# Hybrid attention block on one core: the order of four engines written out for the start of the kernel, extra matmuls while data arrive, mask building moved behind the last weight split

## The chip, the cores and the metric

The kernel runs on one core of one Trainium2 chip. The metric is the device time of one execution, in microseconds. The kernel before takes 1032.24 us (median of 3 runs, 1032.16 to 1032.51).

## The reference

One decoder block on 512 tokens of width 1024, all in float32:

```
h    = RMSNorm(x)                      # over 1024, gain norm1_g
proj = h @ W_in                        # 1024 x 9744
A    = dilated attention, 3 groups of 8 heads of 64; q and k are RMS-normed per head
B    = gated linear attention, 4 heads, output norm, swish gate
mix  = sigmoid(gA) * (A @ W_A) + sigmoid(gB) * (B @ W_B)
x    = x + mix @ W_out
x    = x + relu(RMSNorm(x) @ W_up)^2 @ W_down
```

Only the very beginning matters here: `RMSNorm(x)`, and the first 512 columns of `W_in`, which are the queries of attention group 0, followed by their normalisation per head (`q = q * rsqrt(mean(q^2) + eps)`), while the keys of group 0, the next 512 columns at `kind * 1536`, are multiplied.

## The kernel before

**Precision.** Each float32 factor is split into a high part (`hi`, a copy rounded to fp32r by ScalarE, line 110) and a low part (`lo = raw - hi`, line 111). A product is three matmuls: hi*hi, hi*lo, lo*hi (lines 155 to 157 with a whole projection's loop around them). So each weight piece of 128 x 1024 needs one ScalarE copy `whi` and one subtraction `wlo`. For the first four pieces `wlo` is made by GpSimd, for all later ones by VectorE. `whi` and `wlo` have four buffers each, the raw weights `wraw` two.

**Tiles.** The 512 tokens are four tiles of 128 (`i` = 0..3). A projection by `mm_tok` has four PSUM banks of the tag `mm`, one per token tile, and goes over 8 blocks of 128 rows of the weight: 8 x 4 x 3 = 96 matmuls of 512 columns. The tag `mm` has five banks in all, the tag `aux` three.

**The beginning, per token tile `i`.** `square_in`: ScalarE squares x and sums. `rsqrt`: a chain of small steps, VectorE (`rv`), ScalarE (`ry`, logarithm and exponential), VectorE (`r`). `scale_in`: VectorE multiplies x by `r` and the gain, in two halves. The gain row is spread over the partitions by two TensorE matmuls (`g1b`). `turn_in`: TensorE transposes h, 8 times 128 x 128. `parts_in`: ScalarE copies the high part `hTh` from PSUM, VectorE subtracts for the low part `hTl`. Beside it `split_in` makes `whi` and `wlo` of the first projection's four weight pieces. In this stretch the order on ScalarE and VectorE is as the program writes it (`manual_schedule`); TensorE and GpSimd are ordered by the scheduler's own estimate.

**Constants.** The block behind `issue_after(last.ins)` loads small columns by GpSimd DMAs and builds the attention masks and the masks of the gated attention on GpSimd. It may be issued only once `last`, the last low part of h, has been scheduled; on GpSimd the scheduler then laid it between the `wlo` of the first projection.

**After the first projection** (`qkv`, kind 0, that is q): per token tile ScalarE copies the bank to `rw` (which frees the bank), GpSimd squares it (`s2`, line 346), VectorE sums per head (`ss`), then the `rsqrt` chain, VectorE scales (`s2` again), and four transposes (`turn`, line 357) go into TensorE's order while the next projection (k) is under way, the first of them after 48 of its 96 matmuls.

**What sets the order.** Each engine takes its instructions in one fixed order and waits on semaphores. The build fixes that order; from the first projection's end on it is the scheduler's.

Of the kernel before, what the change touches and what calls it, by code (L numbers as in the profile page):

```python
# [8 lines left out]
F32 = mybir.dt.float32  # L9
# [7 lines left out]
P = 128  # L17
# [24 lines left out]
def kernel(ctx: ExitStack, tc: tile.TileContext, x, norm1_g, w_in, q_g, k_g,  # L42
# [54 lines left out]
        return t  # L97


    n_split = [0]  # L100
    first = []
    later = []
    turns = []

    def split(raw_ap, shape):
        hi = ring.tile([P] + shape, F32R, name="whi", tag="whi")
        lo = ring.tile([P] + shape, F32R, name="wlo", tag="wlo")
        n_split[0] += 1
        with tc.high_priority() if n_split[0] > 4 else nullcontext():
            act(hi, raw_ap, AF.Copy)  # L110
            (nc.vector if n_split[0] > 4 else nc.gpsimd).tensor_tensor(lo, raw_ap, hi.bitcast(F32), OP.subtract)  # L111
        return hi, lo

    def raw_load(w, r0, nk, c0, n):
# [29 lines left out]
    def mm_tok(w, c0, lhs, r0=0, nk=KB):  # L144

        banks = [mm_bank() for _ in range(NT)]
        for k4 in range(0, nk, 4):
            raw = None if first else raw_load(w, r0 + k4 * P, 4, c0, 512)
            for k2 in range(0, 4, 2):
                hi, lo = first.pop(0) if raw is None else split(raw[:, k2:k2 + 2], [2, 512])  # L150
                for kk in range(2):
                    k = k4 + k2 + kk
                    for i in range(NT):
                        lh, ll = lhs(k, i)
                        nc.tensor.matmul(banks[i], lh, hi[:, kk], start=(k == 0), stop=False)  # L155
                        nc.tensor.matmul(banks[i], lh, lo[:, kk], start=False, stop=False)  # L156
                        mm = nc.tensor.matmul(banks[i], ll, hi[:, kk], start=False, stop=(k == nk - 1))  # L157
                    if later and k in (3, 4, 5, 6):
                        with tc.issue_after(mm.ins):
                            later.pop(0)()  # L160
        return banks
# [34 lines left out]
    raws = [slot(10 + j, [P, 4, 512], f"raw{j}") for j in range(2)]  # L196


    def load_x(i):
        nc.sync.dma_start(xs[i // 2][:, i % 2], x[i * P:(i + 1) * P])  # L200

    def load_in(j):
        nc.sync.dma_start(raws[j // 2][:, j % 2 * 2:j % 2 * 2 + 2],
                          w_in[2 * j * P:2 * (j + 1) * P, 0:512].rearrange("(k p) n -> p k n", p=P))

    g1r = slot(8, [P, D], "g1r")[0:1]
    nc.scalar.dma_start(g1r, norm1_g)
    for i in range(NT):
        load_x(i)
        load_in(i)  # L210

    one_r = small.tile([1, P], F32, name="one_r", tag="one_r", bufs=1)
    nc.vector.memset(one_r, 1.0)
    g1b = [mm_bank(), aux()]
    for j in range(2):
        nc.tensor.matmul(g1b[j], one_r, g1r[:, j * 512:(j + 1) * 512], start=True, stop=True)

    ss4 = consts.tile([P, 4], F32, name="ss4")
    r4 = consts.tile([P, 4], F32, name="r4")

    def square_in(i):
        act(hs[i // 2][:, i % 2], xs[i // 2][:, i % 2], AF.Square, accum_out=ss4[:, i:i + 1])

    def scale_in(i):
        for j in range(2):
# [1 line left out]
            nc.vector.scalar_tensor_tensor(hs[i // 2][:, i % 2, cs], xs[i // 2][:, i % 2, cs], r4[:, i:i + 1],  # L227
                                           g1b[j], op0=OP.mult, op1=OP.mult)

    def turn_in(i):  # L230
        bs = [aux() for _ in range(2)]
        for k in range(KB):
            nc.tensor.transpose(bs[k // 4][:, k % 4 * P:(k % 4 + 1) * P], hs[i // 2][:, i % 2, k * P:(k + 1) * P],
                                ident)
        return [b.rearrange("p (k t) -> p k t", k=4) for b in bs]

    def parts_in(i, bs):
        for j in range(2):
            dh = hT.hi[j][:, :, i * P:(i + 1) * P]
            act(dh, bs[j], AF.Copy)  # L240
            last = tt(hT.lo[j][:, :, i * P:(i + 1) * P], bs[j], dh.bitcast(F32), OP.subtract)
        return last

    def split_in():
        j = len(first)
        first.append(split(raws[j // 2][:, j % 2 * 2:j % 2 * 2 + 2], [2, 512]))

    with tc.manual_schedule(engines={mybir.EngineType.Activation, mybir.EngineType.DVE}):
        square_in(0)
        rsqrt(r4[:, 0:1], ss4[:, 0:1], D, 1)  # L250
        scale_in(0)
        split_in()
        square_in(1)
        rsqrt(r4[:, 1:2], ss4[:, 1:2], D, 1)
        b0 = turn_in(0)
        scale_in(1)
        parts_in(0, b0)
        split_in()
        square_in(2)
        square_in(3)  # L260
        rsqrt(r4[:, 2:4], ss4[:, 2:4], D, 2)
        b1 = turn_in(1)
        scale_in(2)
        parts_in(1, b1)
        split_in()
        b2 = turn_in(2)
        scale_in(3)
        parts_in(2, b2)
        split_in()
        last = parts_in(3, turn_in(3))  # L270


    with tc.issue_after(last.ins):
        qk_cols = consts.tile([P, 2], F32, name="qk_cols")
        for j, g in enumerate((q_g, k_g)):
            for hf in range(2):
                nc.gpsimd.dma_start(qk_cols[hf * E:(hf + 1) * E, j:j + 1], g.rearrange("o e -> e o"))
        gqk = consts.tile([P, 1], F32, name="gqk")
        nc.vector.scalar_tensor_tensor(gqk, qk_cols[:, 0:1], float(E) ** -0.5, qk_cols[:, 1:2],
                                       op0=OP.mult, op1=OP.mult)  # L280

        gqk2 = consts.tile([P, 2], F32, name="gqk2")
        nc.vector.memset(gqk2, 0.0)
        for hf in range(2):
            nc.vector.tensor_copy(gqk2[hf * E:(hf + 1) * E, hf:hf + 1], gqk[hf * E:(hf + 1) * E])

        mask_a = consts.tile([P, 256], F32, name="mask_a")
        nc.gpsimd.memset(mask_a, 0.0)
        nc.gpsimd.affine_select(mask_a[:, :P], mask_a[:, :P], pattern=[[1, P]], compare_op=OP.is_ge,
                                fill=NEG, base=0, channel_multiplier=-1)  # L290
        nc.gpsimd.affine_select(mask_a[:, P:], mask_a[:, P:], pattern=[[-1, P]], compare_op=OP.is_ge,
                                fill=NEG, base=0, channel_multiplier=1)
        mask_b = consts.tile([P, 256], F32, name="mask_b")
        nc.gpsimd.tensor_copy(mask_b[:, :P], mask_a[:, P:])
        dist = t2k(P, "dist", I32)
        nc.gpsimd.iota(dist, pattern=[[1, P]], base=P, channel_multiplier=-1)
        nc.vector.tensor_single_scalar(dist, dist, 3, op=OP.bitwise_and)
        far = t2k(P, "far")
        nc.vector.tensor_copy(far, dist)
        nc.vector.tensor_scalar(far, far, 0.5, NEG, op0=OP.is_gt, op1=OP.mult)  # L300
        tt(mask_b[:, P:], far, mask_a[:, P:], OP.min)


        def block_mask(name, w, segs):

            g = consts.tile([P, w], U8, name=name)
            f = work_e.tile([P, w], F32, name="f", tag="s2", bufs=2)
            nc.gpsimd.memset(f, 1.0)
            for off, ng, nx, gr, r0, nr in segs:
                v = f[:, off:off + ng * nx].rearrange("p (g x) -> p g x", x=nx)  # L310
                nc.gpsimd.affine_select(v, v, pattern=[[-gr, ng], [0, nx]], compare_op=OP.is_ge, fill=0.0,
                                        base=-r0, channel_multiplier=1)
                nc.gpsimd.affine_select(v, v, pattern=[[gr, ng], [0, nx]], compare_op=OP.is_ge, fill=0.0,
                                        base=r0 + nr - 1, channel_multiplier=-1)
            nc.gpsimd.tensor_copy(g, f)
            return g

        pair_mask = {m: block_mask(f"pm{m}", 256, [(64 * i, 64 // m, m, 2 * m, 0, m) for i in range(NT)])
                     for m in (1, 32)}
        quad_mask = {}  # L320
        for m in (2, 8):
            G = 32 // m
            quad_mask[m] = block_mask(f"qm{m}", 384, [
                (192 * i + off, G, (3 - a) * m, 4 * m, a * m, m)
                for i in range(2) for a, off in enumerate((0, 96, 160))])
        gbias = col("gbias", gate_bias, GH)
        og_col = col("og_col", out_g, 2)
        bb_col = col("bb_col", branch_bias, 16)
        n2_col = col("n2_col", norm2_g, KB)
        nbb_col = consts.tile([P, 16], F32, name="nbb_col")  # L330
        nc.vector.tensor_scalar_mul(nbb_col, bb_col, -1.0)


    def qkv(g, lhs, sq, sk, sv):
# [1 line left out]

        res = []
        for kind, ss_ in ((0, sq), (1, sk)):
            banks = mm_tok(w_in, kind * 1536 + g * 512, lhs)
            dst = [slot(s, [P, 4, S], f"a{kind}{g}{n}") for n, s in enumerate(ss_)]  # L340
            for i in range(NT):
                rw = work_e.tile([P, 512], F32, name="rw", tag="rw", bufs=4)
# [584 lines left out]
```

## Time and profile before

| | |
|---|---|
| median of 3 runs | 1032.24 us |
| profiled execution: its time, its span | 1034.02 us, 1032.3 us |
| TensorE busy | 1012.2 us, 98% |
| VectorE, ScalarE, GpSimd busy | 64%, 49%, 8% |
| TensorE on the chain that ended last | 92% |

TensorE is nearly always busy, and where it is not, is almost all in the first 21 us. A time line row gives the start, the duration, the engine, the source line, the operation with its output and inputs, and in brackets the idle time of that engine just before and what ended it. A row "x3" merges three alike instructions that follow each other; its duration is that of all three. Matmuls overlap, so the pace is read from their starts, not from their durations.

### The profile page before, as it was taken

Reading aid. Unit: us, or ns where it says so; the run is one execution under the profiler, and the core shown is the slowest. Engines: PE = TensorE matmul, PEld = TensorE weight load, DVE = VectorE, ACT = ScalarE, POOL = GpSimd, SP = SyncE. Lnnn points to the kernel's source line nnn. Section 1 sums busy time; section 2 is a strip of 40 time slices with the busy share of each in tenths; the row PEclk is TensorE's granted clock in tenths of the full one; section 3 lists DMA queues with packets and bytes.
Section 4 is the critical chain, followed back from the end, with each engine's and each line's share of the span. In section 5 each row is a group of like instructions: output and inputs, shape, how many; then the busy total and the mean of one; then the engine's idle time right before and its main releaser. Section 6 shows DMA issues by size and latency. Waiting matters only on the chain.

```text
span 1032.3 us, 12479 instructions
## 1 busy us (share of the span) xinstructions
PE 1012.2 (98%) x4772; PEld 860.3 (83%) x4772; DVE 665.7 (64%) x1109; ACT 507.3 (49%) x845; POOL 81.8 (8%) x116
## 2 busy tenths in 40 slices
PE   5999999999999999999999999999999999999998
PEld 3888999999988788788888888777888888888886
DVE  5654454435444623989856657985885895796695
ACT  4345443433544423765646863365544554563552
POOL 7510001001000000010002200000000000000000
PEclk8999999999999999999999999999999999999999
DMA  6132102332201223212212334252143134225102
GB/s 244 45 109 93 42 5 78 96 109 82 82 12 34 92 69 116 82 43 80 64 60 85 120 123 163 79 207 82 42 156 114 57 98 146 83 82 163 41 1 81
DMA packets 63788, 91.84 MB, mean 89 GB/s; under 512 B 3249, under 2 KB 37041, under 8 KB 63730
## 3 DMA queue, kind: packets, MB, share of 16 engines
q1 hardware_dynamic: 61520, 87.59, 25.6%
q10 hardware_dynamic: 1794, 3.18, 0.9%
q8 instruction: 37, 0.61, 0.2%
q0 software_dynamic: 416, 0.28, 0.2%
q14 instruction: 21, 0.17, 0.1%
HBM read 88.92 MB, written 2.13 MB: 88 GB/s over the span
## 4 chain that ended last, share of the span: by engine, by line
PE 92%; DVE 4%; ACT 1%; POOL 1%; issue 1%; DMA 0%; SPq 0%; POOLq 0%; DVEq 0%
PE mm L136 11%; PE mm L137 10%; PE mm L138 10%; PE mm L155 10%; PE mm L157 9%; PE mm L156 9%; PE mm L759 4%; PE mm L758 4%; PE mm L760 4%; PE aux L400 3%; PE aux L759 2%; PE aux L760 2%; PE aux L758 2%; PE aux L423 1%; PE aux L394 1%; PE aux L409 1%
## 5 line engine op out<-in xcount | busy, mean ns | idle before, releaser
L111 DVE TENSOR_TENSOR wlo<-wraw,whi 128x1024 fp32r<-128x1024 f32 x127 | 157.5, 1240 | 145.7 <-ACT whi L78 144.0
L78 ACT ACTIVATE whi<-wraw 128x1024 fp32r<-128x1024 f32 x127 | 134.3, 1057 | 189.5 <-PE mm L157 85.5
L155 PE MATMUL mm<-whi,hTh 128*128 128x512 f32 x416 | 172.0, 414 | 1.6 <-ACT hTh L78 1.5
L156 PE MATMUL mm<-wlo,hTh 128*128 128x512 f32 x416 | 167.1, 402 | 3.8 <-POOL wlo L111 3.8
L157 PE MATMUL mm<-whi,hTl 128*128 128x512 f32 x416 | 168.1, 405 | 0.0
L156 PEld LDWEIGHTS mm<-wlo,hTh 128*128 128x128 f32 x416 | 103.0, 248 | 12.7 <-POOL wlo L111 4.2
L155 PEld LDWEIGHTS mm<-whi,hTh 128*128 128x128 f32 x416 | 102.8, 247 | 10.8 <-ACT hTh L78 2.3
L157 PEld LDWEIGHTS mm<-whi,hTl 128*128 128x128 f32 x416 | 102.6, 247 | 9.0
L136 PE MATMUL mm<-xgh,whi 128*128 128x512 f32 x240 | 93.4, 389 | 0.0
L137 PE MATMUL mm<-xgl,whi 128*128 128x512 f32 x240 | 93.4, 389 | 0.0
L138 PE MATMUL mm<-xgh,wlo 128*128 128x512 f32 x240 | 93.4, 389 | 0.0
L758 PE MATMUL mm<-whi,left 128*128 128x512 f32 x200 | 78.0, 390 | 0.7 <-ACT whi L78 0.7
L759 PE MATMUL mm<-wlo,left 128*128 128x512 f32 x200 | 77.8, 390 | 0.5 <-DVE wlo L111 0.5
L136 PE MATMUL mm<-hTh,whi 128*128 128x512 f32 x192 | 77.6, 404 | 0.0
L760 PE MATMUL mm<-whi,left 128*128 128x512 f32 x200 | 77.2, 389 | 0.0
L137 PE MATMUL mm<-hTl,whi 128*128 128x512 f32 x192 | 76.4, 398 | 0.0
L138 PE MATMUL mm<-hTh,wlo 128*128 128x512 f32 x192 | 76.3, 398 | 0.0
L78 ACT ACTIVATE whi<-traw 128x1024 fp32r<-128x1024 f32 x40 | 42.3, 1058 | 46.1 <-PE mm L760 22.3
L81 DVE TENSOR_TENSOR left<-tmp,left 128x256 fp32r<-128x256 f32 (+1 forms) x40 | 43.2, 1089 | 22.8 <-ACT left L78 22.6
L78 ACT ACTIVATE p<-p,nmx 128x256 f32<-128x256 f32 (+1 forms) x64 | 31.2, 488 | 51.3 <-DVE nmx L388 51.3
L396 DVE COPY pt<-aux 128x512 f32<-128x512 f32 (+1 forms) x32 | 21.1, 659 | 54.8 <-PE aux L394 54.6
L136 PEld LDWEIGHTS mm<-xgh,whi 128*128 128x128 f32 x240 | 45.0, 188 | 9.4
(249 smaller groups left out, 1892.8 us busy)
## 6 DMA issues: line engine op xcount, KB each, us to landing
wraw<-in_w_in_dram SPq DMA_DIRECT2D x36, 1024.0 KB, 5.0
wraw<-in_w_ff_up_dram SPq DMA_DIRECT2D x16, 1024.0 KB, 5.3
traw<-in_w_ff_down_dram SPq DMA_DIRECT2D x12, 1024.0 KB, 5.5
wraw<-in_w_gla_branch_dram SPq DMA_DIRECT2D x4, 1024.0 KB, 5.0
wraw<-in_w_ff_down_dram SPq DMA_DIRECT2D x4, 1024.0 KB, 5.0
traw<-in_w_out_dram SPq DMA_DIRECT2D x3, 1024.0 KB, 6.9
x<-in_x_dram SPq DMA_DIRECT2D x4, 512.0 KB, 7.6
raw<-in_w_in_dram SPq DMA_DIRECT2D x4, 512.0 KB, 8.0
```

Of the source, the lines that this page charges most:

```text
L78: nc.scalar.activation(o, i, f, **kw)
L81: return nc.vector.tensor_tensor(o, a, b, op)
L111: (nc.vector if n_split[0] > 4 else nc.gpsimd).tensor_tensor(lo, raw_ap, hi.bitcast(F32), OP.subtract)
L136: nc.tensor.matmul(b, hi[:, k], rh, start=(k == 0), stop=False)
L137: nc.tensor.matmul(b, hi[:, k], rl, start=False, stop=False)
L138: mm = nc.tensor.matmul(b, lo[:, k], rh, start=False, stop=(k == nk - 1))
L155: nc.tensor.matmul(banks[i], lh, hi[:, kk], start=(k == 0), stop=False)
L156: nc.tensor.matmul(banks[i], lh, lo[:, kk], start=False, stop=False)
L157: mm = nc.tensor.matmul(banks[i], ll, hi[:, kk], start=False, stop=(k == nk - 1))
L758: nc.tensor.matmul(banks[i], lh, hi[:, jk], start=f, stop=False, skip_group_check=True)
L759: nc.tensor.matmul(banks[i], lh, lo[:, jk], start=False, stop=False, skip_group_check=True)
L760: nc.tensor.matmul(banks[i], ll, hi[:, jk], start=False, stop=l, skip_group_check=True)
```

## The change

The order of all four compute engines is written out until the last `wlo` of the first projection, that projection included (`first_mm`); `mm_tok` no longer has a special case for it. The four x tiles are loaded ahead of the weights on SyncE's queue, with the first weight piece on ScalarE's queue. 25 matmuls of 256 columns whose results are not read (`keep_busy`) stand before the gain's matmuls (15) and between the first two transposed tiles (10). `g1b` takes two `mm` banks. The first `wlo` is made by VectorE, the other three by GpSimd, one after the other. The block of constants and masks waits for the last of these three (`last_g`) as well.

```diff
     def split(raw_ap, shape):
...
-        n_split[0] += 1
-        with tc.high_priority() if n_split[0] > 4 else nullcontext():
+        with tc.high_priority():
             act(hi, raw_ap, AF.Copy)
-            (nc.vector if n_split[0] > 4 else nc.gpsimd).tensor_tensor(lo, raw_ap, hi.bitcast(F32), OP.subtract)
+            tt(lo, raw_ap, hi.bitcast(F32), OP.subtract)
...
     nc.scalar.dma_start(g1r, norm1_g)
+    load_in(nc.scalar, 0)
     for i in range(NT):
-        load_x(i)
-        load_in(i)
-
+        nc.sync.dma_start(xs[i // 2][:, i % 2], x[i * P:(i + 1) * P])
+    for j in (1, 2, 3):
+        load_in(nc.sync, j)
...
+    def keep_busy(n, b):
+
+        for m in range(n):
+            nc.tensor.matmul(b[:, :256], busy[:, m % 4 * P:m % 4 * P + P], busy[:, :256], start=True, stop=True)
...
+    def split_in(j, eng):
+        raw = raws[j // 2][:, j % 2 * 2:j % 2 * 2 + 2]
...
+        act(hi, raw, AF.Copy)
+        first_w.append((hi, lo))
+        return eng.tensor_tensor(lo, raw, hi.bitcast(F32), OP.subtract)
...
+    with tc.manual_schedule(engines={ET.Activation, ET.DVE, ET.Pool, ET.PE}):
+
+        g1b = [mm_bank(), mm_bank()]
+        first_banks = [mm_bank(), mm_bank()]
+        keep_busy(15, first_banks[1])
+        for j in range(2):
+            nc.tensor.matmul(g1b[j], one_r, g1r[:, j * 512:(j + 1) * 512], start=True, stop=True)
         square_in(0)
-        rsqrt(r4[:, 0:1], ss4[:, 0:1], D, 1)
+        rsq(0, 1)
         scale_in(0)
-        split_in()
         square_in(1)
-        rsqrt(r4[:, 1:2], ss4[:, 1:2], D, 1)
-        b0 = turn_in(0)
+        b0 = turn_in(0, [aux(), aux()])
+        high_in(0, b0)
+        rsq(1, 2)
         scale_in(1)
-        parts_in(0, b0)
-        split_in()
+        keep_busy(10, first_banks[1])
+        b1 = turn_in(1, [aux(), mm_bank()])
+        low_in(0, b0)
+        split_in(0, nc.vector)
         square_in(2)
+        high_in(1, b1)
+        low_in(1, b1)
+        first_mm(0, [0])
+        first_mm(1, [0])
         square_in(3)
-        rsqrt(r4[:, 2:4], ss4[:, 2:4], D, 2)
-        b1 = turn_in(1)
+        rsq(2, 4)
+        split_in(1, nc.gpsimd)
         scale_in(2)
-        parts_in(1, b1)
-        split_in()
-        b2 = turn_in(2)
+        b2 = turn_in(2, [aux(), aux()])
+        high_in(2, b2)
         scale_in(3)
-        parts_in(2, b2)
-        split_in()
-        last = parts_in(3, turn_in(3))
-
-
-    with tc.issue_after(last.ins):
+        low_in(2, b2)
+        b3 = turn_in(3, [aux(), mm_bank()])
+        first_banks += [mm_bank(), mm_bank()]
+        first_mm(0, [1])
+        first_mm(1, [1])
+        split_in(2, nc.gpsimd)
+        high_in(3, b3)
+        last = low_in(3, b3)
+        last_g = split_in(3, nc.gpsimd)
+        first_mm(2, [0, 1])
+        first_mm(3, [0, 1])
+        for j in (2, 3):
+            for i in range(NT):
+                first_mm(i, [j])
+
+
+    with tc.issue_after(last.ins), tc.issue_after(last_g.ins):
         qk_cols = consts.tile([P, 2], F32, name="qk_cols")
...
-            banks = mm_tok(w_in, kind * 1536 + g * 512, lhs)
+            banks = first_banks if kind == g == 0 else mm_tok(w_in, kind * 1536 + g * 512, lhs)
```

The rest of the kernel stands as before. What the new code does to three places of the built order:

On GpSimd, at the start of the kernel, before (`wlo` is a low part of the first projection's weights, the rest are constants and masks):

```order
masks.py:199 AFFINE_SELECT ident<-ident 128x128
L111 TENSOR_TENSOR wlo<-raw_97,whi 128x1024
L277 DMA qk_cols<-in_attn_q_norm_g_dram 64x1
L277 DMA qk_cols<-in_attn_k_norm_g_dram 64x1 x2
L288 MEMSET mask_a 128x256
L296 IOTA dist 128x128
L289 AFFINE_SELECT mask_a<-mask_a 128x128
```

The same place now:

```order
masks.py:199 AFFINE_SELECT ident<-ident 128x128
L256 TENSOR_TENSOR wlo<-raw_97,whi 128x1024
L256 TENSOR_TENSOR wlo<-raw_98,whi 128x1024 x2
L320 DMA qk_cols<-in_attn_q_norm_g_dram 64x1 x2
L320 DMA qk_cols<-in_attn_k_norm_g_dram 64x1 x2
L331 MEMSET mask_a 128x256
L339 IOTA dist 128x128
```

The three `wlo` that GpSimd still has stand ahead of all mask work, where before there were four, spread through it.

On GpSimd, ahead of the first square of q (`s` <- `rw`), before:

```order
L96 DMA n_col<-in_norm_g_dram 128x8x1
L313 AFFINE_SELECT f<-f 128x64
L313 AFFINE_SELECT f<-f 128x32
L315 CAST qm_296<-f 128x384
L111 TENSOR_TENSOR wlo<-raw_98,whi 128x1024
L346 TENSOR_TENSOR s_427<-rw 128x512
```

The same place now:

```order
L354 AFFINE_SELECT f<-f 128x32
L96 DMA n_col<-in_norm_g_dram 128x8x1
L356 AFFINE_SELECT f<-f 128x64
L356 AFFINE_SELECT f<-f 128x32
L358 CAST qm_425<-f 128x384
L389 TENSOR_TENSOR s_456<-rw 128x512
```

What stands directly ahead of the square of q is now the last mask, and no longer the last `wlo`.

On ScalarE, where the first projection ends (`whi` <- `wraw` belongs to the k projection, `rw` <- `mm` frees a bank of q, `ry` is the chain of the normalisation of q's first token tile), before:

```order
L78 ACTIVATE whi<-wraw 128x1024 x3
L78 ACTIVATE rw<-mm 128x512 x3
L78 ACTIVATE ry<-rv 128x8
L78 ACTIVATE rw<-mm 128x512
L78 ACTIVATE whi<-wraw 128x1024
L78 ACTIVATE ry<-ry 128x8
```

The same place now:

```order
L78 ACTIVATE whi<-wraw 128x1024 x3
L78 ACTIVATE rw<-mm 128x512 x2
L78 ACTIVATE ry<-rv 128x8
L78 ACTIVATE ry<-ry 128x8
L78 ACTIVATE rw<-mm 128x512 x2
L78 ACTIVATE whi<-wraw 128x1024
```

Two copies of q's banks stand ahead of the `ry` chain now, where before there were three.

## Rows read from the trace of the kernel before

**Rows 1.** Page, parts 1 and 4: engines, and the chain that ended last.

```profile
PE 1012.2 (98%) x4772; PEld 860.3 (83%) x4772; DVE 665.7 (64%) x1109; ACT 507.3 (49%) x845; POOL 81.8 (8%) x116
PE 92%; DVE 4%; ACT 1%; POOL 1%; issue 1%; DMA 0%; SPq 0%; POOLq 0%; DVEq 0%
```

**Rows 2.** Time line of TensorE (start us, us, ... [idle before <- releaser]).

```profile
13.45 1.12 PE L233 MATMUL aux<-ident,h 128*128 128x128 f32 x4 [0.92 <-DVE hTl L81]
...
16.77 0.40 PE L155 MATMUL mm<-whi,hTh 128*128 128x512 f32 x1
20.96 0.80 PE L156 MATMUL mm<-wlo,hTh 128*128 128x512 f32 x1 [3.79 <-POOL wlo L111]
...
35.45 0.39 PE L156 MATMUL mm<-wlo,hTh 128*128 128x512 f32 x1
...
46.11 0.39 PE L155 MATMUL mm<-whi,hTh 128*128 128x512 f32 x1
...
56.99 0.60 PE L357 MATMUL aux<-ident,s 128*128 128x128 f32 x4
```

**Rows 3.** Windows of 1 us: busy per engine, granted clock, DMA share, GB/s.

```profile
20.00:21.00 1.00, 0.04 (x1) 0.04 (x1) 0.97 (x2) 0.17 (x1) 1.00 (x2) 0.50 0.01 2
...
26.00:27.00 1.00, 1.00 (x7) 0.95 (x6) 0.69 (x1) 0.32 (x2) 1.00 (x4) 0.59 0.00 0
27.00:28.00 1.00, 1.00 (x6) 0.78 (x5) 0.45 (x1) 1.00 (x2) 1.00 (x4) 1.00 0.00 0
```

**Rows 4.** Time line of GpSimd, 0 to 50 us.

```profile
1.36 0.73 POOL L277 DMA_DIRECT2D qk_cols<-in_attn_q_norm_g_dram  x1 [0.35 <-issue]
...
9.57 0.55 POOL L277 DMA_DIRECT2D qk_cols<-in_attn_q_norm_g_dram  x1
...
18.55 2.36 POOL L111 TENSOR_TENSOR wlo<-raw,whi 128x1024 fp32r<-128x1024 f32 x1
20.85 0.40 POOL L315 CAST pm<-f 128x256 uint8<-128x256 f32 x1
...
28.34 1.19 POOL L96 DMA_DIRECT2D bb_col<-in_branch_gate_bias_dram  x1
...
30.91 2.38 POOL L111 TENSOR_TENSOR wlo<-raw,whi 128x1024 fp32r<-128x1024 f32 x1
33.26 1.09 POOL L313 TENSOR_SCALAR_AFFINE_SELECT f<-f 128x96 f32<-128x96 f32 x4
...
36.67 2.39 POOL L111 TENSOR_TENSOR wlo<-raw,whi 128x1024 fp32r<-128x1024 f32 x1
44.94 2.04 POOL L346 TENSOR_TENSOR s<-rw 128x512 f32<-128x512 f32 x2 [5.88 <-ACT rw L78]
```

**Rows 5.** Time line of ScalarE, 0 to 50 us.

```profile
8.96 1.06 ACT L78 ACTIVATE h<-x 128x1024 f32<-128x1024 f32 x1 [1.77 <-DMA x<-in_x_dram]
...
10.67 1.07 ACT L78 ACTIVATE hTh<-aux 128x512 fp32r<-128x512 f32 x2
11.62 1.06 ACT L78 ACTIVATE whi<-raw 128x1024 fp32r<-128x1024 f32 x1
...
17.82 0.20 ACT L78 ACTIVATE ry<-rv 128x2 f32<-128x2 f32 x1 [2.64 <-DVE rv L184]
...
44.27 1.96 ACT L78 ACTIVATE rw<-mm 128x512 f32<-128x512 f32 x3 [2.29 <-PE mm L157]
47.04 0.21 ACT L78 ACTIVATE ry<-rv 128x8 f32<-128x8 f32 x1 [0.82 <-DVE rv L184]
47.16 0.58 ACT L78 ACTIVATE rw<-mm 128x512 f32<-128x512 f32 x1
```

**Rows 6.** Time line of VectorE, 0 to 50 us.

```profile
11.38 0.75 DVE L227 SCALAR_TENSOR_TENSOR h<-x,r,mm 128x512 f32<-128x512 f32 x1
...
12.70 1.29 DVE L81 TENSOR_TENSOR hTl<-aux,hTh 128x512 fp32r<-128x512 f32 x2
...
34.60 1.23 DVE L111 TENSOR_TENSOR wlo<-wraw,whi 128x1024 fp32r<-128x1024 f32 x1
```

More of the change, by code (lines that the diff above doesn't have):

```diff
@@ L97, in col @@
         return t
-    n_split = [0]
-    first = []
     later = []
@@ L147, in mm_tok @@
         for k4 in range(0, nk, 4):
-            raw = None if first else raw_load(w, r0 + k4 * P, 4, c0, 512)
+            raw = raw_load(w, r0 + k4 * P, 4, c0, 512)
             for k2 in range(0, 4, 2):
-                hi, lo = first.pop(0) if raw is None else split(raw[:, k2:k2 + 2], [2, 512])
+                hi, lo = split(raw[:, k2:k2 + 2], [2, 512])
                 for kk in range(2):
@@ L196, with load_in, rsq @@
     raws = [slot(10 + j, [P, 4, 512], f"raw{j}") for j in range(2)]
[L199 to L204, printed above, removed]
+    def load_in(eng, j):
+        eng.dma_start(raws[j // 2][:, j % 2 * 2:j % 2 * 2 + 2],
+                      w_in[2 * j * P:2 * (j + 1) * P, 0:512].rearrange("(k p) n -> p k n", p=P))
     g1r = slot(8, [P, D], "g1r")[0:1]
     nc.scalar.dma_start(g1r, norm1_g)
+    load_in(nc.scalar, 0)
     for i in range(NT):
-        load_x(i)
-        load_in(i)
+        nc.sync.dma_start(xs[i // 2][:, i % 2], x[i * P:(i + 1) * P])
+    for j in (1, 2, 3):
+        load_in(nc.sync, j)
     one_r = small.tile([1, P], F32, name="one_r", tag="one_r", bufs=1)
     nc.vector.memset(one_r, 1.0)
-    g1b = [mm_bank(), aux()]
-    for j in range(2):
-        nc.tensor.matmul(g1b[j], one_r, g1r[:, j * 512:(j + 1) * 512], start=True, stop=True)
+    busy0 = slot(9, [P, 512], "busy0")
+    nc.vector.memset(busy0, 1.0)
+    busy = slot(12, [P, 512], "busy", F32R)
+    nc.vector.tensor_copy(busy, busy0)
     ss4 = consts.tile([P, 4], F32, name="ss4")
     r4 = consts.tile([P, 4], F32, name="r4")
+    first_w = []
+    def keep_busy(n, b):
+        for m in range(n):
+            nc.tensor.matmul(b[:, :256], busy[:, m % 4 * P:m % 4 * P + P], busy[:, :256], start=True, stop=True)
     def square_in(i):
         act(hs[i // 2][:, i % 2], xs[i // 2][:, i % 2], AF.Square, accum_out=ss4[:, i:i + 1])
+    def rsq(a, b):
+        rsqrt(r4[:, a:b], ss4[:, a:b], D, b - a)
     def scale_in(i):
@@ L228, in scale_in, with turn_in @@
                                            g1b[j], op0=OP.mult, op1=OP.mult)
-    def turn_in(i):
-        bs = [aux() for _ in range(2)]
+    def turn_in(i, bs):
         for k in range(KB):
@@ L235, in turn_in, with high_in @@
         return [b.rearrange("p (k t) -> p k t", k=4) for b in bs]
-    def parts_in(i, bs):
+    def high_in(i, bs):
         for j in range(2):
-            dh = hT.hi[j][:, :, i * P:(i + 1) * P]
-            act(dh, bs[j], AF.Copy)
-            last = tt(hT.lo[j][:, :, i * P:(i + 1) * P], bs[j], dh.bitcast(F32), OP.subtract)
-        return last
[L244 to L248, printed above, removed]
+            act(hT.hi[j][:, :, i * P:(i + 1) * P], bs[j], AF.Copy)
@@ new lines, in low_in @@
+    def low_in(i, bs):
+        for j in range(2):
+            sl = slice(i * P, (i + 1) * P)
+            last = tt(hT.lo[j][:, :, sl], bs[j], hT.hi[j][:, :, sl].bitcast(F32), OP.subtract)
+        return last
+    def split_in(j, eng):
+        raw = raws[j // 2][:, j % 2 * 2:j % 2 * 2 + 2]
+        hi = ring.tile([P, 2, 512], F32R, name="whi", tag="whi")
+        lo = ring.tile([P, 2, 512], F32R, name="wlo", tag="wlo")
+        act(hi, raw, AF.Copy)
+        first_w.append((hi, lo))
+        return eng.tensor_tensor(lo, raw, hi.bitcast(F32), OP.subtract)
@@ new lines, in first_mm @@
+    def first_mm(i, js):
+        for j in js:
+            hi, lo = first_w[j]
+            for kk in range(2):
+                k = 2 * j + kk
+                lh, ll = hT.nat(k, i)
+                nc.tensor.matmul(first_banks[i], lh, hi[:, kk], start=(k == 0), stop=False)
+                nc.tensor.matmul(first_banks[i], lh, lo[:, kk], start=False, stop=False)
+                nc.tensor.matmul(first_banks[i], ll, hi[:, kk], start=False, stop=(k == KB - 1))
+    ET = mybir.EngineType
+    with tc.manual_schedule(engines={ET.Activation, ET.DVE, ET.Pool, ET.PE}):
+        g1b = [mm_bank(), mm_bank()]
+        first_banks = [mm_bank(), mm_bank()]
+        keep_busy(15, first_banks[1])
+        for j in range(2):
+            nc.tensor.matmul(g1b[j], one_r, g1r[:, j * 512:(j + 1) * 512], start=True, stop=True)
```

## The prediction

> **What bounds the kernel now.** I read the page's engine part and its chain first: TensorE is busy for 98% of the span and makes up 92% of the chain that ended last [rows 1]. So a change counts only by what it does to TensorE's order, and the question is at which time TensorE reaches a given matmul. Next I read TensorE's time line of the beginning. It waits 3.79 us for a low part of GpSimd's and starts in earnest at 20.96; from there it is never idle again in the stretch I looked at. From the matmul at 35.45 to the first one of the k projection at 46.11 there are 47 matmuls, 0.227 us each, and 48 more lead to q's first transposes at 56.99 [rows 2]. [...] Fourth, GpSimd's time line, for the reason of that wait: the second `whi` was done at 12.7 [rows 5], its `wlo` started only at 18.55, because mask work stood ahead of it in GpSimd's order [rows 4]. That wait is what the change removes. Fifth, ScalarE's time line where q ends: three copies from 44.27, then the `ry` of the normalisation, then the fourth copy [rows 5]. There I find what takes its place.
>
> **Part 1, the beginning, up to the last transposes.** I follow the new order by hand, with durations from the rows. The chain starts with the second x tile. It landed at 8.96 [rows 5]; now it is issued earlier, but still third in line behind the first x tile and a weight piece, so I keep 8.96 (nearest row; if it came right behind the first two, two or three us earlier, the next x tiles become the limit, and I put the gain at 1 us). Square and accumulator read, about 1.15: 10.1. Two `hTh`, 1.07 [rows 5]: 11.1; two `ry`, 0.2 each with their gaps: 11.5; three short VectorE steps: 12.1. From there VectorE is the limit: two scalings 1.3 (11.38 to 12.70 [rows 6]), two `hTl` 1.2 to 1.3, the first `wlo`, now VectorE's, 1.23 [rows 6], two `hTl` again: 17.0. The `rsqrt` of tiles 2 and 3 takes 1.25 (end of the square at 10.1 to the first scaling at 11.38): 18.2. Four scalings 2.6: 20.9, four transposes: 21.4. From there TensorE has 84 of q's 96 matmuls left and runs through: 84 x 0.227 = 19.1, so k would start at 40.5 in place of 46.11 [rows 2]: 5.6 us gained so far.
>
> The 25 unread matmuls: one of 512 columns takes 0.227 at the upper clock, so one of 256 at the lower clock takes that too: 15 of them 3.4 us, from about 2 to 5.5. The gain's matmuls behind them end some 1.5 us later than now, and the first tile's scaling with them; this costs nothing, since ScalarE then waits for the second x tile anyway, 1.77 us before 8.96 [rows 5]. If that tile came early, up to 1.5 us would show. The ten later ones stand where TensorE waits for the second tile.
>
> **Part 2, GpSimd.** Its first `wlo` follows the second `whi`, which stands behind `ry` on ScalarE: 17.5 to 18.6. So `wlo` 18.6 to 20.9, the next from 21.8 (its `whi` comes after the third tile's `hTh`), the last 24.1 to 26.4, at 2.30 each (18.55 to 20.85 [rows 4]). Only then does the mask block start. What it takes is the sum of its three stretches between the `wlo` in [rows 4]: 9.57 to 18.55 is 8.98, 20.85 to 30.91 is 10.06, 33.26 to 36.67 is 3.41, and the one DMA that ran ahead, 0.73: 23.2 us. It ends at 26.4 + 23.2 = 49.6. Behind it on GpSimd stands the square of q's first tile, which was ready to go at 37 (the first bank ends 18 matmuls before q does, at 36.4, and a copy takes 0.58).
>
> **Part 3, the new wait.** Who waits for this square? VectorE's sum, then `ry` on ScalarE, and behind `ry` on ScalarE now stand the third and the fourth copy of q's banks. Before, three copies stood ahead of it. The k projection needs four of five `mm` banks: the free one and those of q's tiles 0, 1 and 2. Tile 2's copy is the one that has moved behind `ry`. So TensorE does nine matmuls of k (40.5 to 42.5) and stops for the tenth. From the square's start to `ry` was 44.94 to 47.04 = 2.10 [rows 4, 5]; a second `ry` 0.21, the next copy 0.12 later (47.04 to 47.16), 0.58 long: 3.0. TensorE goes on at 49.6 + 3.0 = 52.6, after 10 us idle. Before, the tenth matmul of k stood at 46.11 + 9 x 0.227 = 48.15. **That is 4.5 us later than before.** The transposes of q, 39 matmuls further, find their input ready by then.
>
> **Part 4, the clock after it.** After 3.8 us of idleness the clock was at the lower level [rows 2, 3]; after 10 us I expect the same. The way back took 5.9 us of matmuls from 20.96, and 3.3 us from 13.45, where the pace reaches the upper level at 16.77 [rows 2]. Half of it is lost: 2.95 or 1.65; I take 2.2.
>
> **What does not count.** The banks of `g1b` and the split's rewriting change no later instruction; `nbb_col` on VectorE now waits for `bb_col`, whose DMA stands 6 us before the masks' end (28.34 to 36.67 without the `wlo` at 30.91 [rows 4]), so it is done before the square, and so is the k weight's `wlo` behind it. Whatever follows hangs on TensorE and moves with it; I know of no later wait that would absorb the shift.
>
> **Sum.** 4.5 + 2.2 = 6.7 us. The profiled execution took 1034.02 (span 1032.3 and 1.7 around it) and would come to 1040.7. It is 1.8 above the median of the runs, 1032.24; against that I predict **1038.9 us**.
>
> **Bounds.** The last `wlo` may end 1 us earlier (x tiles) or 2.2 us later, if the clock is at the lower level when the twelve early matmuls and 16 transposes run (they are then on ScalarE's way to the last `whi`). The masks ran beside VectorE's `wlo` in places; two of these now fall into them, and if each stopped GpSimd for its length, 2 x 1.23 [rows 6] come on top; in [rows 4, 6] the `wlo` at 34.60 was not stretched beside the masks, so I take 0. Worked out from these: 1037.3 to 1044.3.
>
> [...]
>
> **Rivals.** (a) *The gain is kept*: the masks are through before q's first copy is, so k starts at 40.5 and nothing stops it: 1032.2 - 5.6 = 1026.6. It decides if the last `wlo` ends by 37 - 23.2 = 13.8. For it speaks that GpSimd is busy for only 8% [rows 1]; against it that the three `wlo` alone take 6.9 and the first cannot start before the third and fourth x tiles are squared. 3%. (b) *The copies do not wait behind `ry`*: then TensorE first waits at q's transposes, due at 40.5 + 48 x 0.227 = 51.4. Their input is ready at 49.6 + 2.1 for the sum, 0.4 for `ry`, and 2.0 for three short steps and a scaling: 54.1. It waits 2.7, net gain 2.9: 1029.3, faster. For it: the bank is needed by one matmul in a long row. Against it: ScalarE took `hTh` only after the `ry` at 17.82, which waited 2.64 us for VectorE [rows 5], although the transposes were done before; and GpSimd's `wlo` waited behind masks [rows 4]. 4%.
>
> [...]
>
> (c) *The clock is not kept up by the unread matmuls*: everything of the forecast, with the last `wlo` 2.2 later: 1041.1. The ten matmuls in the second tile's wait are there, and gaps are under 2 us, so 15%. (d) *Evens out*: x much earlier, masks shorter without `wlo` between, no loss by the clock: within 2 us of before. 4%. The forecast itself: 74%.
>
> **How the numbers follow.** 0.2%, 2 us, is about what a measurement of this kernel can tell from no change. Faster: (a) and (b), 7%. Within 0.2%: (d), 4%. Slower: 89%. The range, 1035.5 to 1042.5, leaves out (a), (b), (d) and the far ends of the bounds.
>
> **What the next profile would show.** Right: GpSimd's first `s` <- `rw` starts at about 50, directly behind a `qm` cast; ScalarE has a gap of 10 us or more between the second and third `rw`, released by VectorE's `rv`; TensorE idle for about 10 us near 42 to 53, with the granted clock at 0.50 behind it; k's first matmul near 40.5. Wrong: no idle time of over 2 us on TensorE after 22, or a third `rw` right behind the second. If the gap is there but the last mask ends before 45 or after 53, the length of the mask block was mis-sized.

## The result, and the profile after

The changed kernel takes 1042.76 us (median of 4 runs, 1042.47 to 1044.82); the kernel before, beside it, 1032.38 (1032.16 to 1033.53). The ratio is 1.010, 95% interval 1.0088 to 1.0112: slower by 10.4 us. 1038.9 was predicted, between 1035.5 and 1042.5. The direction and the mechanism are as predicted; the loss was put too low by 3.9 us. The profiled execution took 1044.82 us, span 1043.0; before's took 1034.02, so the two profiled executions differ by 10.8.

The page after has, in its first and fourth part, against [rows 1]:

```profile
PE 1016.8 (97%) x4797; PEld 865.1 (83%) x4797; DVE 658.4 (63%) x1112; ACT 507.1 (49%) x845; POOL 80.0 (8%) x115
...
PE 89%; POOL 3%; DVE 3%; ACT 2%; issue 2%; DMA 1%; SPq 0%; POOLq 0%; DVEq 0%; ACTq 0%
```

GpSimd works for no longer than before, and its share of the chain rises from 1% to 3%. Where, its time line says (start, duration, line, operation, idle time before and its releaser); it answers to [rows 4]:

```profile
19.48 2.39 POOL L256 TENSOR_TENSOR wlo<-raw,whi 128x1024 fp32r<-128x1024 f32 x1 [18.10 <-ACT whi L78]
23.71 4.76 POOL L256 TENSOR_TENSOR wlo<-raw,whi 128x1024 fp32r<-128x1024 f32 x2 [1.85 <-ACT whi L78]
28.42 1.27 POOL L320 DMA_DIRECT2D qk_cols<-in_attn_q_norm_g_dram  x2
...
32.15 2.75 POOL L354 TENSOR_SCALAR_AFFINE_SELECT f<-f 128x64 f32<-128x64 f32 x3
34.86 2.43 POOL L356 TENSOR_SCALAR_AFFINE_SELECT f<-f 128x64 f32<-128x64 f32 x3
...
52.60 0.50 POOL L358 CAST qm<-f 128x384 uint8<-128x384 f32 x1
53.06 2.03 POOL L389 TENSOR_TENSOR s<-rw 128x512 f32<-128x512 f32 x2
```

The three `wlo` end at 28.42, then the mask block runs without a pause to 53.06, 24.64 us, and only then comes the square of q's first tile. On ScalarE the third and fourth copy stand behind the `ry` that waits for it; against [rows 5], where three copies went in a row:

```profile
39.29 0.60 ACT L78 ACTIVATE rw<-mm 128x512 f32<-128x512 f32 x1 [0.76 <-PE mm L266]
55.16 0.21 ACT L78 ACTIVATE ry<-rv 128x8 f32<-128x8 f32 x1 [15.27 <-DVE rv L181]
55.40 0.21 ACT L78 ACTIVATE ry<-ry 128x8 f32<-128x8 f32 x1
55.51 1.06 ACT L78 ACTIVATE rw<-mm 128x512 f32<-128x512 f32 x2
```

And TensorE, against [rows 2]:

```profile
41.81 0.39 PE L152 MATMUL mm<-whi,hTh 128*128 128x512 f32 x1
...
43.63 0.39 PE L154 MATMUL mm<-whi,hTl 128*128 128x512 f32 x1
56.15 0.79 PE L152 MATMUL mm<-whi,hTh 128*128 128x512 f32 x1 [12.13 <-ACT rw L78]
...
61.36 0.39 PE L152 MATMUL mm<-whi,hTh 128*128 128x512 f32 x1
...
67.53 0.60 PE L400 MATMUL aux<-ident,s 128*128 128x128 f32 x4
```

k starts 4.3 us earlier than before (5.6 were predicted), does nine matmuls, and stands still for 12.13 us for the third `rw`. Its tenth matmul starts at 56.15 in place of 48.15. From there to 61.36 twelve matmuls take 5.21 us; at 0.227 each they would take 2.72: 2.5 us more are lost, and the granted clock says why:

```profile
56.00:60.00 4.00, 3.85 (x9) 3.08 (x10) 3.77 (x10) 1.93 (x5) 0.00 (x0) 0.50 0.05 8
60.00:61.00 1.00, 1.00 (x3) 0.72 (x3) 0.00 (x0) 0.00 (x0) 0.00 (x0) 0.50 0.81 197
61.00:62.00 1.00, 1.00 (x5) 0.86 (x4) 0.00 (x0) 0.00 (x0) 0.00 (x0) 0.87 1.05 389
62.00:64.00 2.00, 2.00 (x10) 1.62 (x10) 0.64 (x1) 1.06 (x1) 0.00 (x0) 1.00 0.57 219
```

(window, then busy time of TensorE, weight loads, VectorE, ScalarE, GpSimd, then the clock: 0.50 is the lower level, and from 56.74 to 60.58 these matmuls start 0.43 us apart.) 8.0 + 2.5 = 10.5 us. q's first transposes stand at 67.53 in place of 56.99, also 10.5 later; nothing behind that takes the shift back.

### The profile page after: what moved, and what is told of

It reads as the page before. It is cut to its first block, busy times and chain, and to the rows that moved or that the text cites. A ratio compares the mean times of both kernels' runs of the same rounds, so it can differ in the third digit from the quotient of the medians.

```text
span 1043.0 us, 12535 instructions
## 1 busy us (share of the span) xinstructions
PE 1016.8 (97%) x4797; PEld 865.1 (83%) x4797; DVE 658.4 (63%) x1112; ACT 507.1 (49%) x845; POOL 80.0 (8%) x115
## 4 chain that ended last, share of the span: by engine, by line
PE 89%; POOL 3%; DVE 3%; ACT 2%; issue 2%; DMA 1%; SPq 0%; POOLq 0%; DVEq 0%; ACTq 0%
PE mm L133 10%; PE mm L134 10%; PE mm L135 10%; PE mm L152 9%; PE mm L154 9%; PE mm L153 9%; PE mm L802 4%; PE mm L801 4%; PE mm L803 4%; PE aux L443 3%; PE aux L802 2%; PE aux L803 2%; PE aux L801 2%; PE aux L466 1%; PE aux L437 1%
## 5 line engine op out<-in xcount | busy, mean ns | idle before, releaser
L81 DVE TENSOR_TENSOR wlo<-wraw,whi 128x1024 fp32r<-128x1024 f32 x127 | 155.2, 1223 | 145.0 <-ACT whi L78 143.2
L152 PE MATMUL mm<-whi,hTh 128*128 128x512 f32 x384 | 158.8, 414 | 12.1 <-ACT rw L78 12.1
L154 PE MATMUL mm<-whi,hTl 128*128 128x512 f32 x384 | 155.3, 404 | 0.0
L153 PE MATMUL mm<-wlo,hTh 128*128 128x512 f32 x384 | 154.3, 402 | 0.0
L152 PEld LDWEIGHTS mm<-whi,hTh 128*128 128x128 f32 x384 | 96.5, 251 | 20.0 <-ACT rw L78 12.6
L154 PEld LDWEIGHTS mm<-whi,hTl 128*128 128x128 f32 x384 | 96.3, 251 | 8.0
L153 PEld LDWEIGHTS mm<-wlo,hTh 128*128 128x128 f32 x384 | 96.7, 252 | 7.4
```

What stands on the lines that cost most here:

```text
L81: return nc.vector.tensor_tensor(o, a, b, op)
```

## The experiments

Eight kernels, each compared with the kernel before, which took 1032.93 us beside experiments 1 to 4 and 1033.02 beside 5 to 8. For the readings below it helps to see one number of each profiled execution beside its time, the start of q's first transposes on TensorE:

| kernel | k's first matmul | masks' end | q's first transposes | profiled time | rest | median |
|---|---|---|---|---|---|---|
| before | 46.11 | 36.67 | 56.99 | 1034.02 | 977.0 | 1032.38 |
| after | 41.81 | 53.06 | 67.53 | 1044.82 | 977.3 | 1042.76 |
| masks late | 41.47 | late | 52.36 | 1027.95 | 975.6 | 1027.59 |
| before, masks late | 41.54 | late | 52.42 | 1027.90 | 975.5 | 1027.78 |
| masks late, no unread | 40.92 | late | 51.80 | 1027.35 | 975.6 | 1027.37 |
| copies first | 39.33 | 50.19 | 55.20 | 1033.87 | 978.7 | 1033.76 |
| no unread | 40.71 | 52.02 | 66.56 | 1042.15 | 975.6 | 1042.48 |
| half the masks late | 41.45 | 43.76 | 59.20 | 1036.06 | 976.9 | 1036.19 |
| more on VectorE, two inputs | 41.80 | 55.40 | 73.89 | 1051.43 | 977.5 | 1048.41 |
| more on VectorE, one input | 41.45 | 51.96 | 68.29 | 1045.37 | 977.1 | 1043.34 |

The rest (profiled time less the transposes' start) is 975.5 to 978.7 in all ten. These are single executions, and those of the kernel before alone spread over 2.1 us (1031.78 to 1033.92). Within about that, the effect of every one of these edits lies ahead of q's first transposes. (The 978.7 still has its lower clock to come, behind the transposes.)

**1. Masks late.** The changed kernel, with the building of the four block masks moved behind k's last square.

```
         mask_b = ...
-        def block_mask(name, w, segs): ...
-        pair_mask = ...
-        quad_mask = ...
...
     q1T, k1T, v1 = qkv(0, hT.nat, (9,), (10, 14), 11)
+    with tc.issue_after(squares_q[7].ins):     # the eighth square of q and k on GpSimd
+        def block_mask(name, w, segs): ...
+        pair_mask = ...
+        quad_mask = ...
```

> The four block masks of the gated attention are built behind the last square of k instead of ahead of the first square of q; nothing else differs from the changed kernel. Theory W (q's square waits on GpSimd behind the masks, the third copy of q's banks waits on ScalarE behind that square's chain, TensorE waits for the bank): the idle of 12 us at k's tenth matmul is gone, k starts at 41.8 as in the changed kernel against 46.11 before, so 1032.3 - 4.3 = 1028. Rival S (the written start itself, with its unread matmuls and the lower clock, costs the time): it stays above 1036.

Measured: 1027.59 us (1027.05 to 1028.37), 0.9948 of before (0.9934 to 0.9963). GpSimd takes the square as soon as its copy is there. On ScalarE the third and fourth copy still stand behind `ry`, as in the changed kernel, but `ry` waits 1.58 us and not 15.27. TensorE has no stop between k's start and the transposes:

```profile
38.27 2.79 POOL L368 TENSOR_TENSOR s<-rw 128x512 f32<-128x512 f32 x2 [3.62 <-ACT rw L78]
```

```profile
41.12 0.21 ACT L78 ACTIVATE ry<-rv 128x8 f32<-128x8 f32 x1 [1.58 <-DVE rv L182]
...
41.48 1.07 ACT L78 ACTIVATE rw<-mm 128x512 f32<-128x512 f32 x2
```

```profile
41.47 0.39 PE L153 MATMUL mm<-whi,hTh 128*128 128x512 f32 x1
...
52.36 0.60 PE L379 MATMUL aux<-ident,s 128*128 128x128 f32 x4
```

The transposes come 15.17 us earlier than in the changed kernel, and the medians differ by 15.17. (That the two agree to the last digit is chance; the two profiled executions differ by 16.87.) With the masks out of the square's way nothing is left of the loss. They stood in its way twice: ahead of it in GpSimd's order, and in its memory, since `f`, in which a mask is built, and the square `s2` share the two buffers of the tag `s2`. The edit takes away both, and no run tells them apart.

**2. Before, masks late.** The same move in the kernel before, whose start is otherwise left as it was.

> The kernel before with the four block masks built behind the last square of k; its start is left to the scheduler. Theory W (masks on GpSimd are what both kernels wait for, at different places): the second low part starts at about 15.3 in place of 18.55, TensorE starts 3 us earlier, about 1029. Rival S': the gain of the masks-late kernel comes from the written order, then this one stays within 1 us of 1032.3.

Measured: 1027.78 us (1027.55 to 1029.77), 0.9954 of before (0.9939 to 0.9969). It is as fast as with the written start. With the masks gone GpSimd makes the second `wlo` at 15.14 in place of 18.55 [rows 4], and the 3.79 us wait of TensorE [rows 2] is gone; k starts at 41.54:

```profile
13.94 1.19 POOL L96 DMA_DIRECT2D bb_col<-in_branch_gate_bias_dram  x1
15.14 2.38 POOL L112 TENSOR_TENSOR wlo<-raw,whi 128x1024 fp32r<-128x1024 f32 x1
```

k starts 4.6 us earlier, more than the 3.4 of this `wlo`. The rest of the way was on VectorE. In the kernel before, the chain that scales the third and fourth token tile also lost time beside GpSimd: its `rv`, 0.16 us in the changed kernel, took 2.57 and came through as GpSimd's selects ended (17.75), and the next step, 18.29 to 20.96, took 2.67 beside the `wlo` of 18.55 [rows 4]. With the masks late they take 2.28 and 0.16, and the third tile's scaling starts at 18.65 in place of 21.50. The rows of the kernel before, VectorE and then GpSimd:

```profile
15.21 2.57 DVE L184 TENSOR_SCALAR rv<-ss 128x2 f32<-128x2 f32 x1 [1.22 <-ACT h L78]
```

```profile
17.11 0.64 POOL L313 TENSOR_SCALAR_AFFINE_SELECT f<-f 128x64 f32<-128x64 f32 x1
```

So a gain at k's start as large as that of the change (4.3 us) is had by taking the masks out of GpSimd's way. The written order, the new order of loads and the unread matmuls bring nothing beside it that these times show.

**3. Masks late, without the unread matmuls.** As 1, and the two `keep_busy` calls left out.

```
-        keep_busy(15, first_banks[1])
...
-        keep_busy(10, first_banks[1])
```

> As the kernel with the masks built late, without the 25 unread matmuls. If they keep the clock up for the first projection, this one is 1 to 2.5 us slower than that kernel (about 1029 to 1030.5). If they only delay the gain's matmuls and with them the first tile, it is 0 to 1.5 us faster (about 1027).

Measured: 1027.37 us (1026.85 to 1029.16), 0.995 of before (0.9933 to 0.9967): no difference from 1. In the traces both things that were expected happen, and they cancel. Without the unread matmuls the gain's four start at 2.35 in place of 5.64, and the tiles come earlier; but q's early matmuls run at the lower pace, 0.43 us from start to start (14.96 to 19.39) where experiment 1 has 0.23 (16.74 to 19.14). The third tile's transposes start at 19.82 here and at 19.95 there.

**4. Copies first.** The changed kernel, with the four copies of q's banks ahead of the first `ry` on ScalarE, so that the banks come free whatever GpSimd does. The masks stay ahead of the square. (The later q and k projections get their four copies first as well, without the `issue_after`.)

```
+            rws = [work_e.tile([P, 512], F32, name="rw", tag="rw", bufs=4) for _ in range(NT)]
             for i in range(NT):
...
                 with tc.high_priority():
-                    act(rw, banks[i], AF.Copy)
+                    copied = nc.scalar.activation(rws[i], banks[i], AF.Copy)
+            if g == kind == 0:
+                ctx_q = tc.issue_after(copied.ins)
...
+            for i in range(NT):
+                rw = rws[i]
...
                 nc.gpsimd.tensor_tensor(s2, rw, rw, OP.mult)
```

> The changed kernel with all four copies of q's banks ahead of the normalisation chain on ScalarE; the masks stay where they are. Theory W: the bank of tile 2 comes free at about 41, TensorE does not stop at k's tenth matmul but at q's first transposes, due at 41.8 + 48 x 0.227 = 52.7, whose input is ready at 57.4 as in the changed kernel; idle 4.7 us, 0.5 us later than before at that point and up to 2.5 us by the lower clock behind it: about 1035. Rival S, or a bank that is not what TensorE waits for: 1042.8 as the changed kernel.

Measured: 1033.76 us (1032.56 to 1035.11), 1.001 of before (1.0001 to 1.002). TensorE does not stop at k's tenth matmul; it goes through to q's transposes and waits there, for the same square:

```profile
49.98 0.39 PE L154 MATMUL mm<-whi,hTl 128*128 128x512 f32 x1
55.20 1.09 PE L405 MATMUL aux<-ident,s 128*128 128x128 f32 x4 [4.83 <-DVE rv L181]
```

That is what the rival (b) describes, made real by the edit. It is 9.0 us faster than the changed kernel and still 6.2 slower than experiment 1. Of the 5.9 between the two profiled executions the trace shows 5.2: the wait of 4.83 and about 2.5 by a lower clock behind it (0.50 from 55 to 60), less 2.1, since in this one trace the start is earlier (k at 39.33).

**5. Half the masks late.** Only the two masks of 384 columns (`quad_mask`) are moved as in 1. This asks whether the loss goes with the masks' end.

> The changed kernel with two of its four block masks (the 128x384 ones) moved behind k's last square; the small DMAs of that stretch stay. They take 8.4 us of the mask block in the changed kernel. Theory W (the time of k's stop goes one for one with the end of the mask block): k goes on near 47.8 in place of 56.2, the stop is still there at about 4 us, the clock behind it is low again: 1042.8 - 8.4 = 1034.4, between 1033.5 and 1035.5. Rival (the loss comes from the clock or from the start, and the stop is only one part): 1037 or more.

Measured: 1036.19 us (1034.25 to 1037.99, 6 runs), 1.0033 of before (1.0022 to 1.0045). The masks end at 43.76, 9.3 us earlier (8.5 for the block and 0.8 for its start, 27.59), and k goes on at 48.79, 7.4 us earlier. The median is 6.6 lower, not 8.4. It lies between the range of theory W and that of the rival, 0.7 above the one and 0.8 below the other, so the time decides for neither. In the trace the stop is still there, 5.14 us long, and what is missing of one for one, 1.9 us, stands on VectorE, which holds `nbb_col` ahead of the sum of the square:

```profile
45.20 0.64 DVE L369 TENSOR_SCALAR nbb_col<-bb_col 128x16 f32<-128x16 f32 x1 [10.46 <-DMA bb_col<-in_branch_gate_bias_dram]
45.76 1.21 DVE L81 TENSOR_TENSOR wlo<-wraw,whi 128x1024 fp32r<-128x1024 f32 x1
46.89 0.67 DVE L386 TENSOR_REDUCE ss<-s 128x8 f32<-128x512 f32 x1
```

The first square was done near 44.8 (two take 2.04 from 43.76), its sum starts at 46.89. With the masks shorter, the column's DMA is the next thing in line.

**6. More on VectorE, two inputs each,** and **7. one input each.** The mask block took 24.64 us in place of 23.2. The six selects shown above took 5.18 us; before, the same six stand in two rows of 1.86, 3.72 in all. Beside them VectorE makes two `wlo` (33.17 to 35.57). These two kernels add eight VectorE instructions in that stretch, whose results are not read.

```
+        with tc.issue_after(last_c.ins):       # behind gqk2
+            for _ in range(8):
+                tt(junk, xs[0][:, 0, :512], xs[0][:, 1, :512], OP.subtract)           # 6
+                nc.vector.tensor_reduce(junk8, xs[0][:, 0, :512] by heads, AX.X, OP.add)   # 7
```

> The changed kernel with eight more subtractions of two SBUF tiles (128x512, results unread) on VectorE beside the masks. In the changed kernel six selects of the mask block took 5.18 us in place of 3.72 beside 2.40 us of VectorE's low parts, 0.61 us lost for each us. Theory L (a VectorE subtraction of two SBUF tiles stops GpSimd's selects): 8 x 0.68 x 0.61 = 3.3 us more on the mask block, and since TensorE waits for its end, 1045 to 1047. Rival (those selects are slow for another reason, their place or their tile): block as before, 24.6 us, and 1042.0 to 1043.5.

> As the run before, but the eight added VectorE instructions read one SBUF tile each (sums over 128x512 to 128x8, results unread). Theory L with two inputs as the condition: the mask block stays at 24.6 us, 1042.0 to 1043.5. Rival (any VectorE work on SBUF stops GpSimd): as with two inputs, 1045 to 1047.

Measured: 6: 1048.41 us (1046.83 to 1051.43), 1.0155 of before (1.0136 to 1.0174); 7: 1043.34 (1043.23 to 1045.37), 1.0102 (1.0085 to 1.0119). In 6 the block takes 27.00 us (28.40 to 55.40), 2.4 more where 3.3 were expected; only six of the eight subtractions fell into it (6 x 0.68 x 0.61 = 2.5), and the build also laid GpSimd's instructions in another order. In 7 it takes 24.37, no more than in the changed kernel. The clearest reading is within 7, GpSimd's rows and then VectorE's:

```profile
31.33 1.89 POOL L358 TENSOR_SCALAR_AFFINE_SELECT f<-f 128x64 f32<-128x64 f32 x3
33.18 3.37 POOL L360 TENSOR_SCALAR_AFFINE_SELECT f<-f 128x64 f32<-128x64 f32 x3
```

```profile
32.33 1.41 DVE L332 TENSOR_REDUCE junk<-x 128x8 f32<-128x512 f32 x2
33.65 2.39 DVE L81 TENSOR_TENSOR wlo<-wraw,whi 128x1024 fp32r<-128x1024 f32 x2
```

Beside the one-input sums (0.9 us of overlap) three selects take 1.89, against 1.86 before; beside the two `wlo` three take 3.37. Two more sums, from 35.96 on, meet a single select at 36.51, which takes 0.65, and 0.64 before. So theory L holds for subtractions of two tiles: they stretch the selects, and these sums do not. That the number of inputs makes the difference is not shown: a sum also writes 8 columns in place of 512, and the `rv` of experiment 2 has one input and was held up for 2.4 us. The time of 6 is over its range, for another reason: its edit also put the DMA of `bb_col` at the end of the block, VectorE stands on `nbb_col` until 57.69, and k goes on 6.0 us later than in the changed kernel, of which the block is 2.3.

```profile
57.69 0.17 DVE L378 TENSOR_SCALAR nbb_col<-bb_col 128x16 f32<-128x16 f32 x1 [10.78 <-DMA bb_col<-in_branch_gate_bias_dram]
```

**8. No unread matmuls.** The changed kernel, masks in place, without the 25.

> The changed kernel without its 25 unread matmuls. If they keep up the clock, the early matmuls and transposes become slower and the last low part of GpSimd's ends later: up to 2.2 us more, 1045. If they do nothing for it, or only delay the first tile: the same or up to 1 us less, 1041.8 to 1043.

Measured: 1042.48 us (1042.03 to 1043.27), 1.0095 of before (1.0079 to 1.011): the same as the changed kernel. The start shows what they do. Changed kernel, then without them:

```profile
2.15 3.57 PE L220 MATMUL mm<-busy 128*128 128x256 f32 x15 [2.15 <-DVE busy L212]
5.65 3.78 PE L275 MATMUL mm<-g1r,one_r 1*128 1x512 f32 x4
9.36 2.03 PE L236 MATMUL aux<-ident,h 128*128 128x128 f32 x8
```

```profile
3.28 3.75 PE L274 MATMUL mm<-g1r,one_r 1*128 1x512 f32 x4 [3.28 <-DMA g1r<-in_norm_g_dram]
8.09 1.94 PE L236 MATMUL aux<-ident,h 128*128 128x128 f32 x8 [1.06 <-DVE h L231]
```

The gain's four matmuls take 3.78 us behind them and 3.75 without: they run no faster, and start 2.4 us later. q's early matmuls run at the lower pace (0.43 us apart) in both traces, from 17.24 to 19.80 and from 15.99 to 18.97.

## Why the prediction was right in kind and too small

**The part that was right.** k stops at its tenth matmul, for the third `rw`, which stands behind `ry`, which waits for a square behind the last mask. From the square to the tenth matmul 3.0 us were predicted, 3.09 measured (53.06 to 56.15). Experiments 1 and 4 each take away one half of the cause, and the stop is gone. k's start was predicted 1.3 us too early (40.5, 41.81); this does not enter the sum, since the stop swallows it.

**The step that failed: when the square starts.** The prediction has the last `wlo` end at 26.4 and the mask block take 23.2 us, so the square at 49.6. Measured: 28.4, 24.6 and 53.06. The trace's 8.0 + 2.5 = 10.5 us stand against 4.5 + 2.2 = 6.7. Of the 3.8 between them the late start of the masks is 2.0, their length 1.4, the clock after the stop 0.3, and the way from the square 0.1.

*The last `wlo`, 2.0 too early.* The chain was hung on the second x tile at 8.96 [rows 5]. It came earlier; ScalarE squares it at 6.31. What limits then is the gain's matmuls, put back by the 15 unread ones: VectorE's second scaling of the first tile starts at 9.46, released by them, and ScalarE's first `hTh` at 10.51 where 10.1 was in the sum.

```profile
6.31 1.04 ACT L78 ACTIVATE h<-x 128x1024 f32<-128x1024 f32 x1
...
10.51 0.60 ACT L78 ACTIVATE hTh<-aux 128x512 fp32r<-128x512 f32 x1 [3.07 <-PE aux L236]
```

The text named the case ("if that tile came early, up to 1.5 us would show") and put nothing for it. It passes down VectorE's list: four scalings at 19.06, not 18.2. Another 0.8 is the clock: in this execution the first matmuls of q run at the lower level (0.50 from 17 to 20, starts 0.43 us apart); in the one of experiment 1 at the upper (0.23 apart), and there, with the scalings also at 19.06, the last `wlo` ends at 27.6. That is the term of rival (c), which was sized at 2.2 and given 15%. It was held unlikely because gaps are under 2 us; that this keeps the clock up no run shows: TensorE's longest gap between its first matmul and these is 1.44 us in both traces (ahead of 16.75 and of 16.74). The remaining 0.3 is spread over small steps.

*The masks, 1.4 too short.* The bound was in the text (up to 2.46 if VectorE's `wlo` stops GpSimd), and 0 was taken, because a `wlo` at 34.60 was not stretched [rows 6]. That row could hardly show it. For 0.87 of its 1.23 us GpSimd's time line of before has a DMA issue beside it, and no instruction on a tile:

```profile
34.73 0.91 POOL L96 DMA_DIRECT2D n_col<-in_norm_g_dram  x1
```

The next `wlo` of VectorE in that trace, while GpSimd made its own from 36.67 on [rows 4], would have shown it:

```profile
36.81 3.34 DVE L111 TENSOR_TENSOR wlo<-wraw,whi 128x1024 fp32r<-128x1024 f32 x1 [0.98 <-ACT whi L78]
```

3.34 in place of 1.23. In this row VectorE's `wlo` ends 1.1 us behind GpSimd's (40.15, 39.06), as if it had begun there. That a `wlo` of VectorE's stops GpSimd for its whole length was the bound's estimate, and the changed kernel does not show it: the selects lost 1.46 us beside 2.40 of VectorE's, which lost nothing itself.

**The range.** With the terms at what they measured the sum is 10.5, and 1032.24 + 10.5 = 1042.7, the time that came. The bounds of the prediction reached to 1044.3, but the range was cut inside them, at 1042.5. Two terms had been put at nothing, the clock of the early matmuls (0 of up to 2.2) and the stretched masks (0 of up to 2.46), and that both might come in part was not counted.

**The rivals.** (a) needed the masks' end ahead of q's first copy; it came 15 us behind it (37.93, 53.06). (b) needs the copies to be ahead of `ry`; experiment 4 is it, at 1033.8 where (b) had 1029.3: the transposes start at 55.20 where (b) had 54.1, and the clock drops behind that wait too, about 2.5 us that (b) did not count. (c) happened in part. (d) did not come: the masks were longer, not shorter, and the clock did cost time.

## What to carry to other kernels

When work is moved behind something on an engine that takes its instructions in the order of the build (ScalarE took the third copy at 55.51, behind `ry`, though the last matmul into its bank had ended at 40.6), look first for what was queued behind the work, and then for what, on other engines, is queued behind that: here masks that could as well be built some 50 us later (from 83.3 in experiment 1, from 31.7 in the changed kernel) held a square, a sum, a copy, a PSUM bank and so TensorE. Putting the work that can wait behind the last of these brought the kernel before to 1027.78 us, some 5 us faster, and the kernel with the written order to the same time, 1027.59. And a row shows that two engines do not disturb each other only if both were at work on tiles at that time; take several.

## What the runs showed of the hardware that was not expected

- VectorE's and GpSimd's work on SBUF tiles stretched each other, in either direction: three selects 1.89 to 3.37 us beside 2.39 of VectorE's `wlo`, a VectorE `wlo` 1.23 to 3.34 beside a GpSimd `wlo`. Sums with one SBUF input did not (1.41 for two, beside selects at their usual pace); a `rv` of two columns, also with one input, did (0.16 to 2.57, beside a row of selects). What decides it these runs do not show.
- The same start does not always run at the same clock: with identical instructions the gain's four matmuls took 3.78 us in five of the six traces with unread matmuls ahead of them, and 1.98 in the one of experiment 4, whose k then starts 2 us earlier. What decides it these runs do not show.
- Of the profile's granted clock, the stretch of these four matmuls reads 1.00 in either case; their durations, a factor of 1.9 apart, say otherwise. In experiment 3 the stretch from 16 to 20 still reads 1.00, with matmuls 0.43 us apart, the lower pace. At the start of the kernel the pace is the better witness.
